# A two-block transformer kernel: 32 modulation units of the first feed-forward taken from TensorE to VectorE

## The chip, the core and the metric

The kernel runs on one core of a Trainium2 chip. The metric is device time of one execution in microseconds (us); the median of three runs is compared.

## What is computed

Two blocks follow each other, each of two layers (a mixer and a feed-forward in each), on x of 256 tokens by 1024 features, with a second stream of 256 context tokens that goes through the same mixers and the first feed-forward. Arithmetic is fp32. All shifts, scales and gates come from a condition vector by a product with a large weight matrix, the modulation; its weights are streamed once, and do not depend on x. Cut to what matters:

```python
def modulation(cond, w_ada, b_ada):
    m = jax.nn.silu(cond) @ w_ada + b_ada      # 1024 -> 6*1024, for x's condition and the context's
    return [t[..., None, :] for t in jnp.split(m, 6, axis=-1)]

def modulate(h, shift, scale):
    return h * (1 + scale) + shift

# one layer of the first block (the context takes the same path with its own condition)
h = modulate(rms_norm(x, norm1_g[i]), sh1, sc1)
x = x + g1 * (jnp.concatenate([out_a, out_b, out_c], axis=-1) @ w_out[i])
x = x + g2 * conv_ffn(modulate(rms_norm(x, norm2_g[i]), sh2, sc2), w_up[i], conv_w[i], conv_b[i], w_down[i])
```

## The kernel before

Features lie on partitions (8 tiles of 128) and tokens along the free axis. An fp32 product is made exact enough by splitting both sides into a high and a low part: ScalarE rounds a weight into wh (L238), VectorE subtracts for wl (L240), and a product is three matmuls, wh with hH, wh with hL and wl with hH (L285, L286, L289). SP issues every weight load (L219, L224). A weight of 1 MB comes as two raw halves w in two buffers; every third one of a feed-forward takes slots of a pool "x8" of 8 KB per partition instead, for its raw or its wh and wl. Three of that pool's seven slots hold xc, hcH and hcL (the context stream) during the first feed-forward; the other four are shared by such weights and by the modulation loads wm.

The first feed-forward works on x and the context together, 512 columns. It has 22 "up" steps (8 weight tiles, four runs of 24 matmuls into the PSUM tile S) and groups of 4, 4, 4, 4, 3, 3 ups with eight "down" steps each (into one of two PSUM tiles acc). After an up, VectorE and ScalarE make the convolution (L991, L993), silu and gate, and gH, gL (L1028, L1029). After a down, VectorE adds acc into x and into xc (L980, two halves).

A modulation unit (i, n) is 1 MB of the weights: two blocks k of 128 input features by 1024 of the 6144 columns of condition pair i; four units n make one of the six vectors j. mod_parts does units on TensorE: per k four matmuls (L410), the padded condition cpad (128 x 32, both conditions in it) stationary and the weights moving, 256 columns each; a sum over units in SBUF (msum, L414, L416); after the fourth unit two transposes (L426) and the bias (L428). With m=2 one call does two units. The first feed-forward does 40 units, 20 calls, in x8 tiles of 1 MB (wm, L366). The second mixers do 8 more, one per call, in half tiles mw (L372).

The order of TensorE and SP is written out in Python: steps are generators, a planner (go) lets a step's later parts follow when a planned cost has passed (yield cost, wait), and spread lays the modulation calls evenly between the main steps. VectorE, ScalarE and GpSimd are ordered by the scheduler, from what each instruction depends on. SP's issues stand in one queue: a load whose slot isn't free holds up those behind it.

Of the kernel before, what the change touches and what calls it, by code (L numbers as in the profile page):

```python
# [11 lines left out]
F32 = mybir.dt.float32  # L12
F32R = mybir.dt.float32r
BF16 = mybir.dt.bfloat16
AF = mybir.ActivationFunctionType
ALU = mybir.AluOpType
# [3 lines left out]
P = 128  # L20
D = 1024
NT = 256
KD = D // P
# [53 lines left out]
            self.pop()  # L77


def spread(main, fill):  # L80

    out, done = [], 0
    for i, u in enumerate(main):
        out.append(u)
        want = len(fill) * (i + 1) // len(main)
        out += fill[done:want]
        done = want
    return out + fill[done:]
# [17 lines left out]
class Stack:  # L106
# [293 lines left out]
    def mod_parts(self, i, n, m, then=None):  # L400


        nc = self.nc
        j, q = divmod(n, 4)
        acc = self.psum("acc", [P, 512])[:, :256]
        ks = range(2 * q, 2 * (q + m))
        ws = [w for a in range(m) for w in self.wm.pop((i, n + a))]
        for k, w in zip(ks, ws):
            for u in range(4):
                nc.tensor.matmul(acc[32 * u:32 * u + 32], lhsT=self.cpad[:, k], rhs=w[:, 256 * u:256 * u + 256],  # L410
                                 start=k == ks[0], stop=k == ks[-1])
        if q == 0:
            self.msum[i, j] = self.mp.tile([P, NT], F32, tag="msum", name="msum", bufs=1)
            nc.scalar.copy(self.msum[i, j], acc)  # L414
        else:
            nc.vector.tensor_tensor(self.msum[i, j], self.msum[i, j], acc, ALU.add)  # L416
        if then is not None:
            then()
        end = q + m == 4
        yield 0.9 * m, WAIT["mod"] if end else 0  # L420
        if not end:
            return
        sb = self.msum.pop((i, j))
        tr = self.psum("tr", [P, 2, 4, 32])
        for t in range(2):
            nc.tensor.transpose(tr[:, t].rearrange("p u v -> p (u v)"), sb[:, P * t:P * t + P], self.ident)  # L426
        b = self.sm(f"sm{i}", "b")[:, KD * j:KD * j + KD].rearrange("p (u t) -> p t u", t=2)
        nc.vector.tensor_tensor(self.mod[i][:, j].rearrange("p (u t) v -> p t u v", t=2),  # L428
                                tr[:, :, :, i // 2 * 2:i // 2 * 2 + 2],
                                b.unsqueeze(3).to_broadcast([P, 2, 4, 2]), ALU.add)  # L430
        yield 0.22, 0

    def mod_units(self, ns, m=1, x8=False, ahead=1):

        ns = ns[::m]

        def load(q):
            for a in range(m if q < len(ns) else 0):
                self.mod_load(ns[q][0], ns[q][1] + a, x8)

        def step(q):
            if q >= ahead:
                yield from self.mod_parts(*ns[q - ahead], m, lambda: load(q))
            else:
                load(q)

        def go(q):
            i, n = ns[q - ahead] if q >= ahead else (0, 0)
            self.go(step(q), f"m{i}.{n + m - 1}" if q >= ahead else None)

        return [lambda q=q: go(q) for q in range(len(ns) + ahead)]
# [254 lines left out]
    def block1(self, l, after):  # L706
        nc, key, line = self.nc, f"sm{l}", self.line
# [4 lines left out]
        t = self.x8("kvqc")  # L712
        kTB, vB = t[:, 0:512], t[:, 512:1024].rearrange("p (k c) -> p k c", k=4)
        qTC = t[:, 1024:2048].rearrange("p (s a t) -> p s a t", s=2, a=2)
        t = self.x8("kvc")
# [3 lines left out]
        u, gk = uv[:, 0], f"gn{l}"  # L719
# [17 lines left out]
        def chunk(ci, post, ss):  # L737
            return [lambda s=s: self.go(self.proj(f"win{l}", ci, s, post), f"c{ci}{s}") for s in ss]
# [6 lines left out]
        def post_bq(c):  # L745
            return lambda acc, s: self.qk(acc, 4, 64, tbq, self.sm(gk, "bq"), s == 0, rsB[:, s, :, c], 2,
                                          qTB[:, s, 2 * c:2 * c + 2])
# [177 lines left out]
        fill = self.fill_a(l)  # L925
        seq = chunk(0, post_bkv, (0,)) + chunk(1, post_bq(0), (0,)) + chunk(0, post_bkv, (1,))
        if l == 0:
            seq += chunk(1, post_bq(0), (1,))
        else:
            seq = seq[:2] + need("n1") + [self.last_loads] + seq[2:]  # L930
# [4 lines left out]
        n = len(streams)  # L935
# [10 lines left out]
        if l == 1:  # L946
            seq += [lambda: self.go(self.ctx2_norm(), "cx")]
        w0 = wouts(0, slice(0, T))
        seq += cc[:2] + need(*bnames) + spread(cc[2:], spread(w0, fill[1]))
        seq += need(*(f"g{s}" for s in streams))  # L950
        seq += need("c_0011", "c_1011")
        for a, b in MOVES[l]:
            seq.insert((a + b) % len(seq), seq.pop(a % len(seq)))
        if l == 1:
            seq = seq[:12] + spread(seq[12:], self.more_units((1, 12, 20)))
        for u_ in seq:
            u_()
        if l == 1:
# [37 lines left out]
    def ffn(self, i, T, streams, after):  # L996


        nc, key = self.nc, f"sm{i}"
# [8 lines left out]
        def up(g, j):  # L1008
            a = j - starts[g]
            if a == 0:  # L1010
                gt[g] = tuple(self.gp.tile([P, groups[g], T], F32R, tag=t, name=t) for t in ("gH", "gL"))
            wh, wl = self.weights(f"wup{i}", j, k=KD)
            ps = self.psum("S", [P, 2, 512])
            for q in streams:
                hH, hL = self.h[q]
                yield from self.mms([ps[:, b, 256 * q:256 * q + 256] for b in range(2)], range(KD),
                         lambda b, k: (wh[:, k, P * b:P * b + P], wl[:, k, P * b:P * b + P]),
                         lambda b, k: (hH[:, k], hL[:, k]))
            c = self.pt.tile([P, 2, 512], F32, tag="pt", name="cgv")
            self.conv(c[:, 0, :T], ps[:, 0, :T], key, j)  # L1020
            nc.scalar.activation(c[:, 0, :T], c[:, 0, :T], AF.Silu)
            if i < 2:
                self.conv(c[:, 1, :T], ps[:, 1, :T], key, KF + j)
                nc.vector.tensor_tensor(c[:, 1, :T], c[:, 0, :T], c[:, 1, :T], ALU.mult)
            else:
                nc.vector.tensor_tensor(c[:, 1, :T], c[:, 0, :T], ps[:, 1, :T], ALU.mult)
            gH, gL = gt[g]
            nc.scalar.copy(gH[:, a], c[:, 1, :T])  # L1028
            (nc.vector if T == 512 else nc.gpsimd).tensor_tensor(gL[:, a], c[:, 1, :T], gH[:, a].bitcast(F32), ALU.subtract)  # L1029
            if j == KF - 1:  # L1030
                self.lnexp()
# [20 lines left out]
                if last:  # L1052
                    self.post_sums(nst[0], y[:, ft], ft, i == 3)

        main = []
        for kind, g, j in self.ffn_order(T):
            if kind == "up":
                main.append(lambda g=g, j=j: self.go(up(g, j)))
            elif g < len(groups) - 1:
                main += [lambda g=g, ft=ft: self.go(down(g, ft, slice(0, T))) for ft in range(KD)]  # L1060
        for u in spread(main, self.fill_f(i)):
            u()
        if i == 0:
            self.prep1(1)
# [275 lines left out]
    def fill_f(self, i):  # L1340

        if i == 0:
            return self.more_units((1, 0, 12), (2, 0, 8), (1, 20, 24), (2, 8, 24), x8=True, m=2)
        return []

    def more_units(self, *parts, **kw):
# [279 lines left out]
```

## Time and profile before

| what | us |
|---|---|
| runs | 1751.69, 1760.24, 1749.96 |
| median | 1751.69 |
| profiled execution | 1754.48 |
| its span | 1752.7 |

The span is what the trace covers; the execution has 1.8 us more around it. Busy shares of the span are 91% for TensorE, 68% for VectorE, 50% for ScalarE and 8% for GpSimd. A busy TensorE is one with a matmul in flight, so 100% does not say that matmuls could not follow faster.

### The profile page before, as it was taken

What the parts mean: (1) busy time and instruction counts of PE and PEld (TensorE: products, weight loads), DVE (VectorE), ACT (ScalarE), POOL (GpSimd) and SP (SyncE); (2) the same over time, 40 slices, a digit from 0 to 9 for tenths busy, and PEclk for the clock granted to TensorE, in tenths of its full rate; (3) what the DMA queues carried; (4) which work ended last, traced back from release to release, by engine and by line L of the source; (5) the groups of instructions that cost most, each with busy time, mean ns of one, the idle gap of its engine ahead of it and who ended that gap; (6) DMA issues with size and microseconds to landing.
All of it is one profiled execution on the core that took longest, in us unless ns stands there. A gap on an engine that the chain in (4) does not pass through costs nothing.

```text
span 1752.7 us, 32334 instructions
## 1 busy us (share of the span) xinstructions
PE 1599.5 (91%) x12604; PEld 1419.1 (81%) x12604; DVE 1188.5 (68%) x2877; ACT 879.1 (50%) x2147; POOL 136.7 (8%) x162
## 2 busy tenths in 40 slices
PE   6999797999999999889888998988979999779997
PEld 5877457989898989788468998976869999479996
DVE  5765886755555545777788777785776567876665
ACT  6344654523242324455546656563556555656563
POOL 1000001000000000010000101000141012330110
PEclk9999998999999999999899999999989999889999
DMA  8344330444545454334334544565554546435552
GB/s 326 107 145 145 125 125 32 146 182 177 219 143 217 168 205 176 131 119 154 133 109 151 195 167 139 175 220 208 197 180 164 196 155 226 174 118 196 170 176 88
DMA packets 67402, 288.36 MB, mean 165 GB/s; under 512 B 7728, under 2 KB 9008, under 8 KB 54960
## 3 DMA queue, kind: packets, MB, share of 16 engines
q1 hardware_dynamic: 65664, 283.91, 46.0%
q10 hardware_dynamic: 1584, 2.38, 0.4%
q8 instruction: 99, 1.62, 0.4%
q14 instruction: 55, 0.45, 0.1%
HBM read 285.21 MB, written 1.05 MB: 163 GB/s over the span
## 4 chain that ended last, share of the span: by engine, by line
PE 61%; DVE 18%; DMA 10%; ACT 7%; issue 3%; POOL 1%; SPq 0%; ACTq 0%; DVEq 0%; POOLq 0%
PE S L285 9%; PE S L286 9%; PE S L289 9%; PE acc L285 8%; PE acc L286 8%; PE acc L289 8%; DVE wl L240 6%; DMA w<-in_wup_dram 5%; PE acc L410 3%; ACT wh L238 2%; DMA w<-in_wdn_dram 2%; DVE ht L529 1%; PE tr L671 1%; DMA wm<-in_wmod_dram 1%; DVE mx L661 1%
## 5 line engine op out<-in xcount | busy, mean ns | idle before, releaser
L240 DVE TENSOR_TENSOR wl<-w,wh 128x384 fp32r<-128x384 f32 (+2 forms) x1010 | 489.1, 523 | 218.5 <-ACT wh L238 190.7
L238 ACT CAST wh<-w 128x384 fp32r<-128x384 f32 (+2 forms) x1010 | 421.3, 475 | 329.4 <-DMA w<-in_wup_dram 94.9
L285 PE MATMUL S<-hH,wh 128*128 128x256 f32 x1408 | 351.3, 287 | 31.0 <-ACT hH L539 17.4
L286 PE MATMUL S<-hL,wh 128*128 128x256 f32 x1408 | 349.2, 285 | 4.7 <-POOL hL L537 4.0
L285 PEld LDWEIGHTS S<-hH,wh 128*128 128x128 f32 x1408 | 271.6, 193 | 36.9 <-ACT hH L539 18.1
L286 PEld LDWEIGHTS S<-hL,wh 128*128 128x128 f32 x1408 | 271.5, 193 | 7.1 <-POOL hL L537 5.0
L285 PE MATMUL acc<-gH,wh 128*128 128x256 f32 (+1 forms) x728 | 209.0, 311 | 9.2 <-DVE xc L980 4.8
L286 PE MATMUL acc<-gL,wh 128*128 128x256 f32 (+1 forms) x728 | 205.3, 306 | 0.0
L289 PE MATMUL S<-hH,wl 128*128 128x256 f32 x1408 | 198.4, 284 | 0.0
L289 PEld LDWEIGHTS S<-hH,wl 128*128 128x128 f32 x1408 | 182.6, 193 | 0.0
L285 PEld LDWEIGHTS acc<-gH,wh 128*128 128x128 f32 x728 | 138.9, 191 | 23.6 <-issue 7.0
L289 PE MATMUL acc<-gH,wl 128*128 128x256 f32 (+1 forms) x728 | 145.7, 306 | 0.0
L286 PEld LDWEIGHTS acc<-gL,wh 128*128 128x128 f32 x728 | 138.9, 191 | 5.5
L991 DVE SCALAR_TENSOR_TENSOR cgv<-S,sm,cgv 128x255 f32<-128x255 f32 (+1 forms) x132 | 74.8, 567 | 67.6 <-ACT cgv L988 67.1
L289 PEld LDWEIGHTS acc<-gH,wl 128*128 128x128 f32 x728 | 110.2, 191 | 6.5
L988 ACT ACTIVATE cgv<-S,sm 128x256 f32<-128x256 f32 (+1 forms) x132 | 82.7, 628 | 47.3 <-PE S L289 47.3
L285 PE MATMUL acc<-wh,hH 128*128 128x256 f32 x344 | 91.2, 296 | 10.4 <-ACT hH L539 8.2
L1029 POOL TENSOR_TENSOR gL<-cgv,gH 128x256 fp32r<-128x256 f32 x66 | 52.2, 791 | 579.5 <-ACT gH L1028 558.7
L980 DVE SCALAR_TENSOR_TENSOR x<-acc,mod,x 128x256 f32<-128x256 f32 x104 | 50.0, 482 | 57.7 <-PE acc L289 57.3
L286 PE MATMUL acc<-wl,hH 128*128 128x256 f32 x344 | 88.1, 287 | 0.0
L286 PE MATMUL S<-hcL,wh 128*128 128x256 f32 x352 | 86.5, 284 | 0.3 <-DVE hcL L540 0.3
L285 PE MATMUL S<-hcH,wh 128*128 128x256 f32 x352 | 86.4, 280 | 0.0
(268 smaller groups left out, 2837.4 us busy)
## 6 DMA issues: line engine op xcount, KB each, us to landing
wm<-in_wmod_dram SPq DMA_DIRECT2D x72, 1024.0 KB, 7.6
w<-in_wup_dram SPq DMA_DIRECT2D x140, 512.0 KB, 3.9
w<-in_wdn_dram SPq DMA_DIRECT2D x56, 512.0 KB, 4.1
mw<-in_wmod_dram SPq DMA_DIRECT2D x48, 512.0 KB, 4.7
w<-in_wup_dram SPq DMA_DIRECT2D x18, 1024.0 KB, 7.5
w<-in_win_dram SPq DMA_DIRECT2D x32, 512.0 KB, 4.0
w<-in_wout_dram SPq DMA_DIRECT2D x16, 512.0 KB, 4.7
w<-in_wqkv_dram SPq DMA_DIRECT2D x16, 512.0 KB, 3.9
```

Of the source, the lines that this page charges most:

```text
L238: self.nc.scalar.copy(h[:, c:d], w[:, c - a:d - a])
L240: self.nc.vector.tensor_tensor(l[:, c:d], w[:, c - a:d - a], h[:, c:d].bitcast(F32), ALU.subtract)
L285: mm(o, lhsT=s[0], rhs=m[0], start=k == ks[0], stop=False)
L286: mm(o, lhsT=s[0], rhs=m[1], start=False, stop=False)
L289: mm(o, lhsT=S(b, k)[1], rhs=M(b, k)[0], start=False, stop=end and k == ks[-1])
L410: nc.tensor.matmul(acc[32 * u:32 * u + 32], lhsT=self.cpad[:, k], rhs=w[:, 256 * u:256 * u + 256], start=k == ks[0], stop=k == ks[-1])
L529: nc.vector.scalar_tensor_tensor(t, self.xs[s][:, ft], A, r, ALU.mult, ALU.mult)
L661: nc.vector.tensor_reduce(mx, S[:, :, :nk], AX.X, ALU.max)
L980: self.nc.vector.scalar_tensor_tensor(x, acc[:, c], self.mods(i, j)[:, ft, s:s + 1], x, ALU.mult, ALU.add)
L988: nc.scalar.activation(out, ps, AF.Identity, scale=cw[:, n + f:n + f + 1], bias=cb[:, f:f + 1])
L991: nc.vector.scalar_tensor_tensor(o[:, :, 1:256], x[:, :, 0:255], cw[:, f:f + 1], o[:, :, 1:256], ALU.mult, ALU.add)
L1029: (nc.vector if T == 512 else nc.gpsimd).tensor_tensor(gL[:, a], c[:, 1, :T], gH[:, a].bitcast(F32), ALU.subtract)
```

## The change

Of the 48 units of the first feed-forward and the second mixers, 32 are now done on VectorE, all within the first feed-forward: (1,8) to (1,23) and (2,8) to (2,23), eight vectors j. mod_vec multiplies each 128 x 1024 block of weights by the condition's column (a number per partition) and adds it to macc, an accumulator of 128 x 1024 in three buffers that had held mw: 56 operations of VectorE (L446), and ScalarE for the first block of a vector (L444, 8 of them). Only one condition is done, the one that this vector needs. After the fourth unit the sum over partitions is made by TensorE: eight matmuls (L452) with 128 columns of macc stationary and two columns of ones moving, then the bias (L454). The planner puts them 8 us of planned cost after the step. The other 16 units stay on TensorE (8 calls of two units). The second mixers have none. spread now counts an up as 4 and a down as 1. The first feed-forward loads 48 units instead of 40. Lines up to 428 of before are one further down in after, later ones 34 to 36.

```diff
--- before.py
+++ after.py
@@ -77,12 +77,13 @@
             self.pop()
 
 
-def spread(main, fill):
-
-    out, done = [], 0
-    for i, u in enumerate(main):
+def spread(main, fill, cost=lambda u: 1):
+
+    out, done, at, all = [], 0, 0, sum(cost(u) for u in main)
+    for u in main:
         out.append(u)
-        want = len(fill) * (i + 1) // len(main)
+        at += cost(u)
+        want = len(fill) * at // all
         out += fill[done:want]
         done = want
     return out + fill[done:]
@@ -429,6 +430,41 @@
                                 tr[:, :, :, i // 2 * 2:i // 2 * 2 + 2],
                                 b.unsqueeze(3).to_broadcast([P, 2, 4, 2]), ALU.add)
         yield 0.22, 0
+
+    def mod_vec(self, i, n):
+
+
+        nc = self.nc
+        j, q = divmod(n, 4)
+        if q == 0:
+            self.msum[i, j] = self.mp.tile([P, 1024], F32, tag="mw", name="macc", bufs=3)
+        acc, v = self.msum[i, j], i // 2 * 2
+        for k, w in zip((2 * q, 2 * q + 1), self.wm.pop((i, n))):
+            if k == 0:
+                nc.scalar.activation(acc, w, AF.Copy, scale=self.cpad[:, k, v:v + 1])
+            else:
+                nc.vector.scalar_tensor_tensor(acc, w, self.cpad[:, k, v:v + 1], acc, ALU.mult, ALU.add)
+        if q < 3:
+            return
+        yield 0, 8
+        tr = self.psum("tr", [P, KD, 2])
+        for t in range(KD):
+            nc.tensor.matmul(tr[:, t], lhsT=acc[:, P * t:P * t + P], rhs=self.ones[:, 0:2], start=True, stop=True)
+        b = self.sm(f"sm{i}", "b")[:, KD * j:KD * j + KD]
+        nc.vector.tensor_tensor(self.mod[i][:, j, :, 0], tr[:, :, 0], b, ALU.add)
+        del self.msum[i, j]
+        yield 1.2, 0
+
+    def mod_vecs(self, ns):
+
+
+        def step(q):
+            if q < len(ns):
+                self.mod_load(*ns[q], True)
+            if q:
+                yield from self.mod_vec(*ns[q - 1])
+
+        return [lambda q=q: self.go(step(q), "m%d.%d" % ns[q - 1] if q else None) for q in range(len(ns) + 1)]
 
     def mod_units(self, ns, m=1, x8=False, ahead=1):
 
@@ -951,8 +987,6 @@
         seq += need("c_0011", "c_1011")
         for a, b in MOVES[l]:
             seq.insert((a + b) % len(seq), seq.pop(a % len(seq)))
-        if l == 1:
-            seq = seq[:12] + spread(seq[12:], self.more_units((1, 12, 20)))
         for u_ in seq:
             u_()
         if l == 1:
@@ -1052,13 +1086,15 @@
                 if last:
                     self.post_sums(nst[0], y[:, ft], ft, i == 3)
 
-        main = []
+        main, cost = [], {}
         for kind, g, j in self.ffn_order(T):
             if kind == "up":
                 main.append(lambda g=g, j=j: self.go(up(g, j)))
+                cost[main[-1]] = 4
             elif g < len(groups) - 1:
                 main += [lambda g=g, ft=ft: self.go(down(g, ft, slice(0, T))) for ft in range(KD)]
-        for u in spread(main, self.fill_f(i)):
+                cost.update((u, 1) for u in main[-KD:])
+        for u in spread(main, self.fill_f(i), lambda u: cost[u]):
             u()
         if i == 0:
             self.prep1(1)
@@ -1340,7 +1376,8 @@
     def fill_f(self, i):
 
         if i == 0:
-            return self.more_units((1, 0, 12), (2, 0, 8), (1, 20, 24), (2, 8, 24), x8=True, m=2)
+            return spread(self.mod_vecs([(i, n) for i in (1, 2) for n in range(8, 24)]),
+                          self.more_units((1, 0, 8), (2, 0, 8), x8=True, m=2))
         return []
 
     def more_units(self, *parts, **kw):
```

TensorE, first feed-forward, before: the end of a down (acc, 512 columns), a call of mod_parts on two units wm, and the next down.

```order
L289 MATMUL acc_6432<-gH_5526,wl_6293 128x512 x2
L410 MATMUL acc_6447<-wm_6152,cpad_103 32x256 x8
L410 MATMUL acc_6447<-wm_6154,cpad_103 32x256 x8
L285 MATMUL acc_6470<-gH_5526,wh_6292 128x512
L286 MATMUL acc_6470<-gL_5527,wh_6292 128x512
```

After, at the end of an up step (S_5983 is its PSUM tile): the column sums of macc_5642 into tr_6080, and the next up.

```order
L287 MATMUL S_5983<-hcL_3463,wh_5835 128x256
L290 MATMUL S_5983<-hcH_3462,wl_5836 128x256 x8
L452 MATMUL tr_6080<-ones_99,macc_5642 128x2 x8
L286 MATMUL S_6124<-hH_3288,wh_5969 128x256
L287 MATMUL S_6124<-hL_3289,wh_5969 128x256
```

The sum stands directly behind the up, and the next up behind the sum.

SP's queue over the same stretch of the program, before: loads of weights w and, in pairs, of modulation units wm.

```order
L224 DMA w_6008<-in_wup0_dram 128x1024
L224 DMA w_6010<-in_wup0_dram 128x1024
L366 DMA wm_6152<-in_wmod2_dram 128x2048
L366 DMA wm_6154<-in_wmod2_dram 128x2048
L224 DMA w_6156<-in_wdn0_dram 128x1024
L224 DMA w_6158<-in_wdn0_dram 128x1024
L224 DMA w_6288<-in_wdn0_dram 128x1024
L224 DMA w_6290<-in_wdn0_dram 128x1024
L224 DMA w_6414<-in_wup0_dram 128x1024
L224 DMA w_6416<-in_wup0_dram 128x1024
```

After:

```order
L367 DMA wm_5793<-in_wmod2_dram 128x2048
L367 DMA wm_5795<-in_wmod2_dram 128x2048
L225 DMA w_5831<-in_wup0_dram 128x1024
L225 DMA w_5833<-in_wup0_dram 128x1024
L367 DMA wm_5957<-in_wmod2_dram 128x2048
L367 DMA wm_5961<-in_wmod2_dram 128x2048
L225 DMA w_5965<-in_wup0_dram 128x1024
L225 DMA w_5967<-in_wup0_dram 128x1024
L367 DMA wm_6101<-in_wmod2_dram 128x2048
L225 DMA w_6106<-in_wdn0_dram 128x1024
```

The pairs have become single loads and pairs in other places, more of them between the weight loads; wm_5957, the last unit of macc_5642, goes into the slot of wh_5835, which the matmuls of S_5983 read almost to their end.

VectorE after the first group of downs, before: residual steps of downs (x, xc) and the pieces of a weight's low part wl.

```order
L980 SCALAR_TENSOR_TENSOR x_90<-acc_4275,mod0_108,x_90 128x256
L980 SCALAR_TENSOR_TENSOR xc_91<-acc_4275,mod0_108,xc_91 128x256
L980 SCALAR_TENSOR_TENSOR x_90<-acc_4294,mod0_108,x_90 128x256
L980 SCALAR_TENSOR_TENSOR xc_91<-acc_4294,mod0_108,xc_91 128x256
L980 SCALAR_TENSOR_TENSOR x_90<-acc_4309,mod0_108,x_90 128x256
L980 SCALAR_TENSOR_TENSOR xc_91<-acc_4309,mod0_108,xc_91 128x256
L240 TENSOR_TENSOR wl_4367<-w_4257,wh_4366 128x384 x2
L240 TENSOR_TENSOR wl_4367<-w_4257,wh_4366 128x256
L240 TENSOR_TENSOR wl_4367<-w_4259,wh_4366 128x384 x2
L980 SCALAR_TENSOR_TENSOR x_90<-acc_4347,mod0_108,x_90 128x256
```

After:

```order
L1014 SCALAR_TENSOR_TENSOR x_90<-acc_4264,mod0_108,x_90 128x256
L1014 SCALAR_TENSOR_TENSOR xc_91<-acc_4264,mod0_108,xc_91 128x256
L1014 SCALAR_TENSOR_TENSOR x_90<-acc_4283,mod0_108,x_90 128x256
L446 SCALAR_TENSOR_TENSOR macc_4203<-wm_4149,cpad_103,macc_4203 128x1024
L241 TENSOR_TENSOR wl_4251<-w_4153,wh_4250 128x384 x2
L241 TENSOR_TENSOR wl_4251<-w_4153,wh_4250 128x256
L241 TENSOR_TENSOR wl_4251<-w_4155,wh_4250 128x384 x2
L241 TENSOR_TENSOR wl_4251<-w_4155,wh_4250 128x256
L1014 SCALAR_TENSOR_TENSOR xc_91<-acc_4283,mod0_108,xc_91 128x256
L1014 SCALAR_TENSOR_TENSOR x_90<-acc_4298,mod0_108,x_90 128x256
L1014 SCALAR_TENSOR_TENSOR xc_91<-acc_4298,mod0_108,xc_91 128x256
```

Between the two halves of the residual of acc_4283 there now stand a step of the modulation and six pieces of a weight.

## Rows read from the trace of the kernel before

**Rows 1.** The page's busy times, whole span.
```profile
PE 1599.5 (91%) x12604; PEld 1419.1 (81%) x12604; DVE 1188.5 (68%) x2877; ACT 879.1 (50%) x2147; POOL 136.7 (8%) x162
```

**Rows 2.** Busy times by stretch: first feed-forward, its tail, second mixers; us.
```profile
330.00:690.00 360.00, 360.00 (x2894) 324.32 (x2896) 193.51 (x378) 124.86 (x262) 0.00 (x0) 1.00 0.49 181
690.00:740.00 50.00, 44.26 (x344) 35.54 (x335) 37.58 (x95) 20.45 (x47) 0.00 (x0) 0.97 0.54 201
740.00:925.00 185.00, 163.44 (x1220) 132.30 (x1220) 146.85 (x396) 99.32 (x253) 4.43 (x6) 0.93 0.39 126
```

**Rows 3.** Busy times by stretch of L410 (mod_parts' matmuls) alone.
```profile
330.00:690.00 360.00, 31.35 (x520) 15.28 (x524) 1.00 0.49 181
690.00:740.00 50.00, 7.53 (x126) 3.36 (x116) 0.97 0.54 201
740.00:925.00 185.00, 9.43 (x128) 3.52 (x128) 0.93 0.39 126
```

**Rows 4.** The same of L426 (mod_parts' transposes), first feed-forward.
```profile
330.00:690.00 360.00, 3.04 (x16) 2.09 (x16) 1.00 0.49 181
```

**Rows 5.** Chain of work that ended last, 640 to 740: start, us, what.
```profile
651.97 0.96 PE S L289 x8
652.93 1.86 PE acc L410 x32
...
705.35 9.22 DMA wm<-in_wmod_dram
714.62 1.07 PE acc L410 x16
```

**Rows 6.** VectorE groups, 330 to 690: busy us, mean ns, idle before.
```profile
L240 DVE TENSOR_TENSOR wl<-w,wh 128x384 fp32r<-128x384 f32 x112 | 59.1, 554 | 66.6 <-ACT wh L238 51.7 <-PE S L289 13.3 <-DMA w<-in_wup_dram 1.7
...
L1024 DVE TENSOR_TENSOR cgv<-cgv 128x512 f32<-128x512 f32 x21 | 14.5, 692 | 0.5
...
L416 DVE TENSOR_TENSOR msum<-msum,acc 128x256 f32<-128x256 f32 x8 | 3.3, 416 | 4.1 <-PE acc L410 4.1
```

**Rows 7.** The chain, two stretches of TensorE in the first mixers.
```profile
198.02 1.09 PE tr L783 x8
...
202.07 1.95 PE tr L834 x16
```

**Rows 8.** The page's group of 128-column weight loads.
```profile
L285 PEld LDWEIGHTS acc<-gH,wh 128*128 128x128 f32 x728 | 138.9, 191 | 23.6 <-issue 7.0
```

**Rows 9.** The chain in the second mixers.
```profile
853.90 1.86 PE acc L410 x16
...
862.86 5.47 DMA w<-in_wout_dram
```

**Rows 10.** SP's timeline in the second mixers: start, us, what it issues.
```profile
828.92 33.83 SPq L372 DMA_DIRECT2D mw<-in_wmod_dram  x6
```

**Rows 11.** Landing of the wm loads (L366), 330 to 740, min/median/max us.
```profile
DMA to landing us min/median/max: 4.7/6.9/13.7
```

**Rows 12.** What SP's queue waited for, 330 to 690: us, times, longest.
```profile
SPq L366 <- PE S L286: 74.4, 5, 17.4
```

**Rows 13.** TensorE's timeline, 286 to 310: start, us, what, idle before.
```profile
290.55 0.58 PE L285 MATMUL acc<-mixH,wh 128*128 128x256 f32 x1 [3.65 <-ACT mixH L266]
...
296.30 0.41 PE L286 MATMUL acc<-mixL,wh 128*128 128x256 f32 x1
296.51 0.41 PE L285 MATMUL acc<-mixH,wh 128*128 128x256 f32 x1
...
298.06 0.28 PE L286 MATMUL acc<-mixL,wh 128*128 128x256 f32 x1
298.18 0.28 PE L285 MATMUL acc<-mixH,wh 128*128 128x256 f32 x1
```

**Rows 14.** VectorE's timeline: two residual steps on end, 372 to 400.
```profile
378.56 0.48 DVE L980 SCALAR_TENSOR_TENSOR x<-acc,mod,x 128x256 f32<-128x256 f32 x1 [0.71 <-PE acc L289]
...
381.38 0.48 DVE L980 SCALAR_TENSOR_TENSOR x<-acc,mod,x 128x256 f32<-128x256 f32 x1 [1.34 <-PE acc L289]
```

## Prediction

> **What bounds the kernel now.** I read the busy shares first: TensorE has 91% of the span, VectorE 68% [rows 1]. Then the busy times by stretch, since the change touches three stretches only. From 330 to 690 us, the first feed-forward, TensorE is busy for 360.00 of 360 us at full granted clock, VectorE for 193.51, ScalarE for 124.86 [rows 2]: TensorE is the bound there, and whatever leaves its queue shortens the program as long as it is never kept waiting. In the tail (690 to 740) it idles for 5.7 us, in the second mixers (740 to 925) for 21.6 of 185 us [rows 2]: there chains of small steps through VectorE, ScalarE and loads bind, and work taken from TensorE counts only where it stands in such a chain.
>
> **What leaves TensorE.** L410 has 520 and 126 instructions up to 740 us, 640 of them being 20 calls of 32 [rows 3]. On the chain of work that ended last such a call takes 1.86 us, behind the last eight matmuls of an up at 0.96 [rows 5]. 12 of 20 calls go: 12 x 1.86 = 22.3 us. Of ten pairs of transposes six go; 16 of them take 3.04 us [rows 4], pipelined somewhat less, so six pairs give 1.4 to 2.3 us; I take 1.4. Together 23.7 us.
>
> **What comes to TensorE.** Eight column sums of eight matmuls each, 128 columns stationary and two moving; an fp32 matmul shows as two instructions, so 16 loads with little behind them. The trace has no such operation. The nearest: 16 instructions of L834 take 1.95 us, eight of L783 (128 columns on 128) take 1.09 us, which is 2.2 for 16 [rows 7]. Lower end: 16 of L410, with 32 columns loaded, at half a call, 0.93 [rows 5]. Upper end: 16 loads at 191 ns with no overlap, 3.1 us [rows 8]. I take 2.0, by L834, the row with as many loads of that width: 8 x 2.0 = 16 us, bounds 7 and 24. The Trainium skill (TensorE: Matmul & The Clock Gate, LDWEIGHTS) puts a load at its columns over 1.2 GHz, 107 ns for 128; by it a sum would be 1.7 us and all eight 13.7; the rows of 1.95 and 2.2 us stand above that, so it isn't used.
>
> The balance of TensorE's own work is thus 16 - 23.7, about **-8 us** (-16 to 0): most of what leaves comes back as sums.
>
> **VectorE.** The 56 new operations are 1024 wide. Forms of 256 and 512 take 416 and 692 ns [rows 6], 276 per 256, so 1024 is 692 + 2 x 276 = 1.24 us, and 56 of them 69.6 us; with the copies and adds of 12 calls gone (at most 0.42 each [rows 6], 5 us) VectorE rises from 193.51 of 360 to about 258, 72%. ScalarE gets eight copies of about the same length, 9 us onto 124.86. Neither becomes a bound as a sum. They cost where something that TensorE needs soon stands behind them in a row.
>
> **Second mixers.** Eight calls (9.43 us busy [rows 3]) and four transposes go, and 16 loads of 512 KB. On the chain there stand calls such as 1.86 us at 853.90, and a wait of 5.47 us for a w_out half [rows 9], which was issued only after six mw loads had held SP's queue for 33.83 us [rows 10]. Were all calls on the chain, 9.4 us and the wait's 5.5 would go; but the chain is mostly that of VectorE and ScalarE, where a call slips into idle time. I take five of eight calls, 5 us, and 2 of the wait (ScalarE is late next): **-7 us** (-3 to -12).
>
> **New waits.** The order of after against the durations above shows six places in the first feed-forward where TensorE must wait. It waited nowhere there.
>
> 1. After the first group of downs, one operation on wm_4149 (1.24 us) and six weight pieces (up to 0.55 each, 3.05 together [rows 6]) stand between the halves of the residual of acc_4283. The third down from there needs that buffer. VectorE needs 4.3 us and two halves; a down takes 2.81 us (378.56 to 381.38 [rows 14]). That leaves about 2.4 us with all data there; the load behind is issued only when the fourth down frees its slot, so I take 2.9.
> 2. The second group, the same with one operation between: 1.0.
> 3. The sum of macc_5076: behind its bias add stand a convolution and the next unit's step, then the six pieces of the next down's weight: 3.2.
> 4. The third group, as 1: 3.0.
> 5. The sum of macc_5642 is the surest. wm_5957 is released when the matmuls of S_5983 on wh end, and the sum stands behind that up, only the eight of 0.96 us [rows 5] between. A wm load lands after 4.7 to 6.9 us [rows 11], then two operations, 2.4 us: 4.7 + 2.4 - 1.0 = 6.1 to 8.3. I take 6.8. Before, such a release cost nothing, though the loads waited for S up to 17.4 us [rows 12], since their call stood far behind.
> 6. The sum of macc_6103: its two loads are freed by the end of a fourth down, and the sum comes 2.3 downs, 6.4 us, later; 6.9 + 2.4 and some pieces of weights make 3.7.
>
> The six are 20.6 us. The clock comes on top: after an idle time of 3.65 us matmuls at 296.30 and 296.51 still follow at 0.21 us, at 298.06 and 298.18 at 0.12 [rows 13], so about 6.5 us ran at the lower level, 1.2 GHz, and cost half of it, 3.2. That falls due after place 5 and perhaps 6. Against it, a wait gives VectorE and SP time that the next place then needn't wait for; I take off 4. **+20 us**, bounds 9 (places 5 and 6 alone, short) and 31 (each at its long end, clock twice).
>
> The tail's 9.22 us on a wm load [rows 5] may shorten, since other loads now end the stretch, or turn into one for w; I put it at nothing, between -5 and +3.
>
> **The sum.** -8 - 7 + 20 = +5 us, on the profiled execution 1754.48 to 1759.5; that execution is 2.8 above the median of the runs, 1751.69, which becomes **1757 us**. The ends: -16 - 12 + 9 - 5 = -24, and 0 - 3 + 31 + 3 = +31. Not all ends come together; the range for this case is -15 to +22, 1737 to 1774. One per cent, 17.5 us, is about what a measurement of this kernel tells from no change.
>
> **Rivals.**
>
> *The waits hardly appear* (0.22): the loads lead by more than I read, and VectorE is ahead by enough. For it: TensorE waited for no wm load in this stretch before, DMA's share is 0.49 [rows 2], and at the other six sums I found the loads early. Against: place 5 can't, by its order. With 4 us left the sum is -8 - 7 + 4 = -11, 1741; with sums at the low end -20, 1732. So the gain passes one per cent only if two bounds are met.
>
> *Slower: the x8 slots become the bound* (0.25). One place and mechanism: a unit's load waits for a slot that a matmul frees, and the sum's position is fixed by planned cost, not by the load. It decides where landing plus two operations, 7 to 9 us, is longer than what the plan puts between release and sum. I see that at two vectors of eight (places 5 and 6); if later loads queue on one another, as wm after wm in SP's order, it is so at five. Each then costs 6.4 us and some 2 of clock: 5 x 8.4 = 42 in place of places 5 and 6 with their clock, 13.7; with the other four places at 10 the sum is -15 + 42 + 10 = +37, **1789**; at four vectors 1780. The Trainium skill (TensorE: Matmul & The Clock Gate, HAM oscillation) tells of kernels in which each wait for a load drops the clock, and the matmuls after it run at half rate. By that every such vector pays, as priced; the rows after the 3.65 us agree [rows 13].
>
> *No gain in the second mixers* (0.13): the chain goes over VectorE and ScalarE whatever TensorE does, and the w_out wait turns into one for the next weight. Then -8 + 0 + 20 = +12, 1764.
>
> **How the numbers follow.** My forecast has 0.40, the rivals 0.22, 0.25 and 0.13. Faster by over 1% (under 1734): two thirds of the first rival's chance falls short of it, which leaves 0.07, and the forecast's low end adds 0.05: 0.12. Slower by over 1% (over 1769): the second rival's 0.23, of the forecast and the third 0.05: 0.28. Within: 0.60. The range takes the first rival in whole down to 1735 and reaches into the second: 1735 to 1780.
>
> **What would show it.** In the profile of after: TensorE idle 9 to 31 us between 330 and 700, most of it before L452 (waiting for VectorE's L446) and before the first matmul of a down (waiting for L1014 or L241); a lower clock just after; L452 at 1.9 to 2.2 us per 16; VectorE near 72% there; L410 256 instructions in that stretch; the second mixers shorter by 3 to 12 us. No idle there would make me wrong to the fast side; L452 waiting at most vectors, to the slow one. What I can't see is how far VectorE's and SP's rows slip together over a stretch that has become fuller for both.

## The result and the profile after

The changed kernel takes 1785.61 us (median of 4 runs, 1776.90 to 1790.83), the kernel before in the same measurement 1755.10 (4 runs, 1749.96 to 1760.24): 1.0161 times as long, 95% interval 1.0134 to 1.0188. It is slower, where 1757 with a range to 1780 was forecast. The profiled execution took 1790.83 us, the slowest of the four, and its span is 1788.9.

To see where the time went I cut the span at three instructions that both kernels have: the first convolution of the first feed-forward, the last addition into the context's residual xc, and the last normalisation product ht of the context, which ends the second mixers. Rows of those lines in the changed kernel; behind the colon are shortest, median and longest duration, then the first and the last start:

```profile
L1025 DVE SCALAR_TENSOR_TENSOR cgv<-S,sm,cgv x132: 470/482/754, 331.1 to 1736.5; 128x255 f32<-128x255 f32 x88, 128x510 f32<-128x510 f32 x44
...
L1014 DVE SCALAR_TENSOR_TENSOR xc<-acc,mod,xc x64: 467/477/489, 221.7 to 775.0; 128x256 f32<-128x256 f32 x64
...
L565 DVE SCALAR_TENSOR_TENSOR ht<-xc,mscale,rstd x32: 476/482/488, 24.2 to 945.9; 128x256 f32<-128x256 f32 x32
```

So the first feed-forward takes 443.9 us (331.1 to 775.0) and the second mixers 170.9 (to 945.9). The same cuts in the kernel before are 415.8 and 168.5: the first feed-forward has become 28.1 us longer, the second mixers have not become shorter. The rest is unchanged, 842.7 and 843.0 us; ahead of the first convolution, where nothing was changed, 5 us differ, which is chance (below).

Busy times by stretch in the changed kernel, in the columns of [rows 2]: window and length, then busy us and number of instructions of TensorE, its weight loads, VectorE, ScalarE and GpSimd, then granted clock, DMA share and GB/s:

```profile
330.00:690.00 360.00, 338.96 (x2477) 312.35 (x2477) 229.46 (x392) 123.13 (x242) 0.00 (x0) 0.97 0.54 196
690.00:760.00 70.00, 63.88 (x477) 57.28 (x476) 55.16 (x113) 27.83 (x59) 0.00 (x0) 0.95 0.51 183
760.00:950.00 190.00, 158.78 (x1054) 131.32 (x1053) 147.61 (x397) 100.42 (x254) 4.41 (x6) 0.87 0.23 76
```

TensorE, busy for all of 360 us before, is idle for 21 of them; VectorE went from 193.51 to 229.46, and the granted clock from 1.00 to 0.97. The window holds less of the stretch than before, since the stretch has become longer. Between the first two cuts, before and changed:

```profile
325.70:741.50 415.80, 410.06 (x3278) 365.66 (x3277) 235.00 (x482) 148.72 (x315) 0.00 (x0) 1.00 0.49 182
331.10:775.00 443.90, 411.92 (x3007) 378.39 (x3006) 296.52 (x538) 157.61 (x317) 0.00 (x0) 0.96 0.51 187
```

VectorE has 61.5 us more to do there, and TensorE is busy for 1.9 us longer with less work (below). Now the idle times. The timeline of TensorE in the changed kernel (start, us, what, and in brackets the idle time before it and what ended it), the eight waits of over 1.3 us before the last steps:

```profile
399.47 0.47 PE L286 MATMUL acc<-gH,wh 128*128 128x512 f32 x1 [2.08 <-DVE xc L1014]
...
457.12 0.44 PE L427 MATMUL tr<-cst,msum 128*128 128x128 f32 x2 [1.40 <-DVE msum L417]
...
534.00 1.26 PE L290 MATMUL acc<-gH,wl 128*128 128x512 f32 x2 [2.44 <-DVE wl L241]
...
557.39 0.47 PE L286 MATMUL acc<-gH,wh 128*128 128x512 f32 x1 [2.94 <-DVE xc L1014]
...
595.52 3.58 PE L452 MATMUL tr<-ones,macc 128*128 128x2 f32 x16 [7.65 <-DVE macc L446]
...
647.44 3.57 PE L452 MATMUL tr<-ones,macc 128*128 128x2 f32 x16 [3.44 <-DVE macc L446]
...
730.57 0.77 PE L286 MATMUL acc<-gH,wh 128*128 128x512 f32 x1 [4.34 <-DVE xc L1014]
...
756.12 0.39 PE L286 MATMUL acc<-gH,wh 128*128 128x256 f32 x1 [1.52 <-DVE x L1014]
```

Five of the six places of the prediction are among them, each with the wait that it named: 2.08 at place 1; 2.44 at 3; 2.94 at 4; 7.65 at 5 and 3.44 at 6. In the group of place 2 the wait for xc is a short one of 0.52 (462.29); the 1.40 there stands before a pair of mod_parts' transposes, which waits for VectorE's sum msum and was not forecast. The last two rows, 4.34 and 1.52, are in the tail group of downs, for which the prediction had put nothing. With two short ones (0.52, 0.56) and the 4.82 us ahead of the last down group (4.83 before as well) the idle time is 31.7 us where it was 5.7.

What TensorE's clock did after the longest wait, in windows of 8 us (column before the last two: granted clock):

```profile
586.00:594.00 8.00, 1.87 (x16) 1.67 (x14) 3.82 (x5) 2.08 (x3) 0.00 (x0) 0.91 0.71 284
594.00:602.00 8.00, 6.48 (x30) 6.48 (x31) 4.94 (x9) 4.04 (x8) 0.00 (x0) 0.50 0.68 241
602.00:610.00 8.00, 8.00 (x66) 8.00 (x65) 4.21 (x8) 0.00 (x0) 0.00 (x0) 0.95 0.80 280
```

For 8 us the granted clock is 0.50, the lower of the two levels, 1.2 GHz. Behind the waits of 2.08, 2.44, 2.94, 3.44 and 4.34 us:

```profile
397.00:405.00 8.00, 5.92 (x37) 5.09 (x36) 6.37 (x12) 1.05 (x3) 0.00 (x0) 1.00 0.93 321
...
533.00:541.00 8.00, 7.00 (x22) 5.42 (x23) 6.79 (x15) 2.42 (x5) 0.00 (x0) 0.79 0.40 131
...
556.00:564.00 8.00, 6.61 (x23) 5.34 (x24) 5.63 (x13) 2.47 (x6) 0.00 (x0) 0.79 0.90 314
...
647.00:655.00 8.00, 7.56 (x28) 6.74 (x29) 4.28 (x11) 2.57 (x5) 0.00 (x0) 0.57 0.88 325
...
729.00:737.00 8.00, 6.43 (x18) 5.09 (x19) 6.81 (x14) 2.93 (x6) 0.00 (x0) 0.57 0.66 229
```

The sum behind the longest wait shows what the lower level makes of it. The chain of work that ended last has sums at both levels, and mod_parts' calls at the price of [rows 5]:

```profile
481.90 1.68 PE tr L452 x16
...
503.76 1.86 PE acc L411 x32
...
528.84 1.69 PE tr L452 x16
...
595.52 3.58 PE tr L452 x16
...
647.44 3.57 PE tr L452 x16
```

VectorE's new operations between 330 and 690 us, 47 of the 56 (form, count, busy us, mean ns, idle before):

```profile
L446 DVE SCALAR_TENSOR_TENSOR macc<-wm,cpad,macc 128x1024 f32<-128x1024 f32 x47 | 60.2, 1281 | 12.6 <-DMA wm<-in_wmod_dram 12.2 <-ACT macc L444 0.2
```

And what SP's queue waited for from 330 to 735 us (us, times, longest): loads of units (L367) stood behind matmuls on weights for 103 us, in nine waits of up to 24.7 us. Before it had been 74.4 us behind S [rows 12] and 31 behind acc, without harm. So the queue does not wait longer for such slots than before; what can differ is how soon the loads are needed, and slots8 and beforeslots below test that.

```profile
SPq L225 <- DVE wl L241: 177.6, 42, 19.3
SPq L367 <- PE acc L287: 59.8, 4, 24.7
SPq L367 <- PE S L287: 43.5, 5, 18.7
```

The acc line before:

```profile
SPq L366 <- PE acc L286: 31.2, 4, 7.8
```

### The profile page after: what moved, and what is told of

Its sections match the earlier page's. It is cut to its first block, busy times and chain, and to the rows that moved or that the text cites. A ratio compares the mean times of both kernels' runs of the same rounds, so it can differ in the third digit from the quotient of the medians.

```text
span 1788.9 us, 31546 instructions
## 1 busy us (share of the span) xinstructions
PE 1605.9 (90%) x12204; PEld 1438.1 (80%) x12204; DVE 1247.5 (70%) x2921; ACT 890.1 (50%) x2149; POOL 138.8 (8%) x162
## 4 chain that ended last, share of the span: by engine, by line
PE 41%; DVE 16%; DMA 9%; ACT 6%; issue 3%; POOL 0%; SPq 0%; ACTq 0%; DVEq 0%; POOLq 0%
PE S L286 7%; PE S L287 7%; PE S L290 7%; DVE wl L241 6%; PE acc L286 5%; PE acc L287 5%; PE acc L290 5%; DMA w<-in_wup_dram 4%; DMA w<-in_wdn_dram 2%; ACT wh L239 2%; DMA wm<-in_wmod_dram 2%; DVE ht L565 1%; DMA w<-in_wqkv_dram 1%; PE acc L411 1%; DVE macc L446 1%
## 5 line engine op out<-in xcount | busy, mean ns | idle before, releaser
L286 PE MATMUL acc<-wh,hH 128*128 128x256 f32 x344 | 92.0, 298 | 10.3 <-ACT hH L575 8.1
```

Source lines behind the costliest of these rows:

```text
L286: mm(o, lhsT=s[0], rhs=m[0], start=k == ks[0], stop=False)
```

## The experiments

The theories. A: what counts are sums that stand too early for their last load, and unit steps in VectorE's row between the halves of a residual. B: VectorE simply has too much to do there. F, formed after the first runs: both are passed on from the loads of the units, which wait in SP's row for an x8 slot that a weight's matmuls hold. For the second mixers, C: the calls taken away had kept TensorE's clock up; D: the chain there never ran over them.

Ratios are to runs of the kernel before on the same chip. The table has each kernel's stretches by the three cuts, from its own profile, and TensorE's idle time in the first feed-forward (sum of the timeline's waits of 0.3 us and more).

| kernel | time, ratio to before (95%) | first feed-forward us | idle us | second mixers us |
|---|---|---|---|---|
| before | 1755.1 | 415.8 | 5.7 | 168.5 |
| again (before once more) | 1764.8, one run | 416.9 | 6.6 | 171.0 |
| after | 1.0161 (1.0134 to 1.0188) | 443.9 | 31.7 | 170.9 |
| late | 1.0106 (1.0071 to 1.0141) | 434.1 | 24.4 | 168.3 |
| narrow | 1.0095 (1.0060 to 1.0130) | 429.4 | 20.3 | 169.1 |
| fillmix | 1.0185 (1.0151 to 1.0220) | 443.6 | 31.8 | 169.4 |
| mixff | 1.0036 (1.0008 to 1.0064) | 427.3 | 8.3 | 164.8 |
| actpool | 1.0344 (1.0287 to 1.0401) | 485.6 | 59.2 | 164.9 |
| costonly | 1761.7, one run | 414.5 | 4.8 | 170.3 |
| resident | 1745.0, one run | 404.4 | 5.8 | 168.5 |
| noroom | 0.9989 (0.9963 to 1.0015) | 407.2 | 11.5 | 169.2 |
| noroom2 | 0.9963 (0.9940 to 0.9986) | 409.9 | 13.3 | 169.3 |
| slots8 | 0.9964 (0.9932 to 0.9996) | 408.4 | 9.4 | 172.2 |
| beforeslots | 1.0026 (1.0005 to 1.0047) | 419.2 | 10.5 | 171.3 |

**late**: the sums later.

```diff
-        yield 0, 8
+        yield 0, 24
         tr = self.psum("tr", [P, KD, 2])
```

> Only the planned time between the last unit of a vector and its column sum is changed, from 8 to 24 us. Theory A (a sum that stands too early for its last load): the two waits of 7.65 and 3.44 us before L452 and the half clock behind them go, two sums take 1.7 instead of 3.6 us; 15 to 20 us less than the changed kernel, about 1768, ratio to before 1.006 to 1.010. Rival B (VectorE has too much to do in the first feed-forward): the waits come back before the downs, 0 to 5 us less, 1781 to 1786.

The two waits before L452 are gone, and 10 us (1.0161 to 1.0106), about half of what theory A gave. The waits before downs stayed, and one behind mod_parts' sum grew (timeline of TensorE, late):

```profile
398.66 0.77 PE L286 MATMUL acc<-gH,wh 128*128 128x512 f32 x1 [2.25 <-DVE xc L1014]
...
458.55 0.44 PE L427 MATMUL tr<-cst,msum 128*128 128x128 f32 x2 [2.18 <-DVE msum L417]
...
538.70 1.27 PE L290 MATMUL acc<-gH,wl 128*128 128x512 f32 x2 [3.29 <-DVE wl L241]
...
719.95 0.77 PE L286 MATMUL acc<-gH,wh 128*128 128x512 f32 x1 [3.89 <-DVE xc L1014]
```

After the wait of 2.18 us at 458.55 the granted clock of the next 8 us is 0.62:

```profile
450.00:458.00 8.00, 6.37 (x63) 4.69 (x61) 6.17 (x12) 2.52 (x5) 0.00 (x0) 1.00 0.56 165
458.00:466.00 8.00, 7.45 (x29) 6.61 (x30) 5.88 (x14) 4.11 (x9) 0.00 (x0) 0.62 0.91 360
```

So waits of 2 us can cost clock too, though not each does: behind the 2.08 us of the changed kernel, and in late behind a wait of 2.94 us at 563.82, the granted clock stayed at 1.00.

```profile
563.00:571.00 8.00, 7.18 (x38) 6.17 (x39) 6.20 (x14) 2.47 (x6) 0.00 (x0) 1.00 0.95 351
```

The two waits that are gone were 11.1 us, but the idle time fell by 7.3 only: the others have grown by 3.8 in sum. The place of the sums explains a third of the loss (9.8 of 28.1 us in the first feed-forward), no more.

**narrow**: VectorE's multiply-adds on 128 of 1024 columns, seven eighths of the product left out.

```diff
-                nc.vector.scalar_tensor_tensor(acc, w, self.cpad[:, k, v:v + 1], acc, ALU.mult, ALU.add)
+                nc.vector.scalar_tensor_tensor(acc[:, :128], w[:, :128], self.cpad[:, k, v:v + 1], acc[:, :128], ALU.mult, ALU.add)
```

> The changed kernel with VectorE's 56 multiply-adds on 128 columns instead of 1024 (so seven eighths of the product are left out); loads, sums and order stay. VectorE has some 54 us less to do in the first feed-forward. Theory A (loads released late, sums placed too early): the wait at macc_5642 stays at 5 us or more, the one at macc_6103 shrinks, and the waits before downs halve: 8 to 15 us less than the changed kernel, 1771 to 1778. Rival B (VectorE's load): all waits of the first feed-forward fall under 2 us in sum, 30 us less, about 1755.

1771.39 us, as theory A said: with VectorE's steps at 349 instead of 1281 ns half of the loss stays, and the wait at the sum of macc_5642 is still 5.79 us, since a load is what it waits for (timeline, narrow):

```profile
587.10 3.57 PE L452 MATMUL tr<-ones,macc 128*128 128x2 f32 x16 [5.79 <-DVE macc L446]
```

Rival B falls as the whole cause.

**fillmix**: eight calls back in the second mixers, without loads, their results unused.

```diff
+                nc.tensor.matmul(acc[32 * u:32 * u + 32], lhsT=self.cpad[:, k],
+                                 rhs=self.blank[:, 256 * u:256 * u + 256], start=k == 0, stop=k == 1)
...
+        if l == 1:
+            seq = seq[:12] + spread(seq[12:], [lambda q=q: self.go(self.idle_unit(q), None) for q in range(8)])
```

> The changed kernel with eight calls of 8 matmuls (128 x 32 stationary, 256 columns) put back into the second mixers, on a constant tile, without loads and with their results unused. Theory C (the calls kept TensorE's clock up there): granted clock from 760 to 950 rises from 0.87 towards 0.93, and the stretch from the last residual of the first feed-forward to the context's last normalisation, 170.9 us now and 168.5 before, is 2 to 6 us shorter in spite of more work. Rival D (the chain runs over VectorE and ScalarE): the stretch is the same or up to 5 us longer, whatever the clock does.

The granted clock from the second cut to the third rose from 0.87 to 0.92, but late had 0.92 there without any such call; the stretch is 169.4 us, within what the others without calls show. Theory C is not borne out: with the calls and the clock back, no gain is seen. Nor is a cost, as D says, but the kernels without calls scatter by 7 us here (below), so one profile can't show that the calls are free.

**mixff**: the kernel before, the mixers' eight units done by TensorE in the first feed-forward.

```diff
-            seq = seq[:12] + spread(seq[12:], self.more_units((1, 12, 20)))
...
-            return self.more_units((1, 0, 12), (2, 0, 8), (1, 20, 24), (2, 8, 24), x8=True, m=2)
+            return self.more_units((1, 0, 24), (2, 0, 24), x8=True, m=2)
```

> The kernel before, with the eight units of the second mixers done by TensorE in the first feed-forward (24 calls of two units there, none in the mixers). Four more calls of 1.86 us cost 7.4 us there. By the prediction's term the mixers give 7 back: ratio 1.000. By the trace of the changed kernel they give nothing or lose 2: ratio 1.004 to 1.006, 1762 to 1765.

The ratio is 1.0036, just under the second figure; its interval (1.0008 to 1.0064) leaves out the first, 1.000. In the profile the first feed-forward is 11.5 us longer and the mixers 3.7 shorter. That looks like half of the predicted gain, but the nine kernels without calls in the mixers lie between 164.8 and 172.2 us, mean 168.6, and the four with them (before, again, costonly, beforeslots) between 168.5 and 171.3, mean 170.3. The gain is about 2 us, from nothing to 4 by this scatter, and no single profile can show it. TensorE's idle time between these cuts scatters less: 25.7 to 27.9 us in the nine, 21.6 to 23.8 in the four, 21.2 in fillmix. So some 4 us of the calls' 9.4 had stood in time that is idle without them. The granted clock there is lower without calls, 0.90 on the average against 0.92 or 0.93 in each of the four, which takes back more.

**actpool**: late, with the products by ScalarE and the additions by GpSimd.

```diff
-                nc.vector.scalar_tensor_tensor(acc, w, self.cpad[:, k, v:v + 1], acc, ALU.mult, ALU.add)
+                nc.scalar.activation(w, w, AF.Copy, scale=self.cpad[:, k, v:v + 1])
+                nc.gpsimd.tensor_tensor(acc, acc, w, ALU.add)
```

> As late, but VectorE has no part in the units: ScalarE multiplies each block in place (56 times some 1.15 us), GpSimd adds it to the accumulator (56 times, some 3 us by the slope of its 256-column adds at 0.79 us). Theory A (a unit's step and its load stand in VectorE's row between the halves of a residual): the waits before downs, 12.9 us in late, go for the most part, and the clock's falls behind them; the first feed-forward 415 to 422 us instead of 434, the whole about 1757 to 1760. Rival E (the x8 slots and SP's row of loads hold everything up): waits of 10 us and more stay, 430 us and over, 1770.

Neither: 1820.59 us, the worst of all. VectorE has none of the units' work, but what it has became slower while GpSimd adds; its pieces of weights, 554 ns in [rows 6], take 737 on the average (groups of actpool by form, 330 to 740). In the trace those that overlap none of GpSimd's additions take 551 ns, the 17 that do 1712 on the average.

```profile
L447 POOL TENSOR_TENSOR macc<-macc,wm 128x1024 f32<-128x1024 f32 x50 | 124.2, 2484 | 305.5 <-ACT wm L446 296.0 <-issue 7.8
...
L241 DVE TENSOR_TENSOR wl<-w,wh 128x384 fp32r<-128x384 f32 x106 | 75.2, 737 | 41.7 <-ACT wh L239 25.0 <-POOL macc L447 16.7
```

Theory A can't be judged by this run, since it brings a cost of its own: waits for wl of up to 5.62 us.

**costonly**: the kernel before with the new weighting of spread (the hunks at spread and at its call in the diff of the change). **again**: the kernel before without an edit.

> The kernel before with only the new weighting of spread (an up counts 4, a down 1). Theory A: nothing is done by VectorE, no wait in the first feed-forward over 1 us, its stretch within 3 us of 415.8. Rival: the weighting puts calls between ups, where their loads or buffers are late, and costs 5 us or more by itself.

> The kernel before, once more, for what varies by itself: the first convolution at 325.7 us in its first profile and at 331 to 332 in all profiles of changed kernels so far, though nothing is changed ahead of it. If that is chance, it comes at 331 here too; the first feed-forward takes 415 to 417 us, the second mixers 167 to 171.

The weighting costs nothing, 414.5 us. And the first convolution comes at 331.8 us in the kernel before too:

```profile
L991 DVE SCALAR_TENSOR_TENSOR cgv<-S,sm,cgv x132: 467/482/751, 331.8 to 1710.1; 128x255 f32<-128x255 f32 x88, 128x510 f32<-128x510 f32 x44
```

So the 5 us ahead of the stretch were chance of the first profile, and they are no part of the change.

**resident**: the changed kernel without VectorE's 32 loads; the steps read hH, so the units' values are meaningless.

```diff
-                self.mod_load(*ns[q], True)
+                self.wm[ns[q]] = [self.h[0][0].rearrange("p k t -> p (k t)")[:, 1024 * e:1024 * e + 1024].bitcast(F32) for e in range(2)]
```

> The changed kernel without its 32 loads of units for VectorE: the multiply-adds read a tile of the hidden state that is there anyway, so these units' values are not the reference's; all instructions of the engines stay. Theory F (what hurts are the loads and the slots they wait for, VectorE's row only passes the wait on): idle of TensorE in the first feed-forward falls from 31.7 us to under 12, its stretch from 443.9 to 410 to 416. Rival B (VectorE's own time, 72 us more): idle stays at 20 us or more, the stretch at 428 or more.

Theory F, and more clearly than expected: all of VectorE's 56 steps are there at their full length, and the idle time is that of the kernel before, 5.8 us. All of TensorE's waits ahead of the last down group (333 to 730 us):

```profile
PE acc L286 <- DVE xc L1014: 0.6, 1, 0.6
PE tr L427 <- DVE msum L417: 0.4, 1, 0.4
PE acc L286 <- DVE x L1014: 0.2, 1, 0.2
```

So the waits before downs came from the loads as well. The stretch is 404.4 us against 415.8 with the same idle time: TensorE's own work has become 11.4 us less.

**noroom** and **noroom2**: late, with the x8 slots left to the units; noroom2 also loads a unit two steps ahead.

```diff
-            plan[n] = name, off, size, extra and (n - base) % 3 == 0, cut
+            plan[n] = name, off, size, extra and (n - base) % 3 == 0 and name[0] not in ("wup0", "wdn0"), cut
```

> As late, and no weight of the first feed-forward takes x8 slots, so the four free slots belong to the units alone and no load of a unit waits for a matmul on a weight; the weights have two buffers of each kind only. Theory F: the waits before downs that come from a late unit go, the first feed-forward 418 to 426 us instead of 434.1, ratio 1.001 to 1.006. Rival G (the weights need the third buffer): TensorE waits for wl or wh instead, 434 us or more.

> As noroom, with a unit loaded two steps ahead of its work instead of one, so that it has landed when VectorE comes to it. Theory F: a few us less again than noroom, 412 to 422 us, ratio 0.998 to 1.004. Rival G: as in noroom, no gain.

Both took the whole loss back, more than either expectation gave: 407.2 and 409.9 us. Loading further ahead adds nothing in the stretch.

**slots8**: the changed kernel with that one line, sums at 8 us. **beforeslots**: the kernel before with it.

> The changed kernel with one edit: no weight of the first feed-forward takes x8 slots; the sums keep their 8 us. Theory F (the slots are the cause, the sums' place only passes it on): loads of units wait for no matmul, so the sums of macc_5642 and macc_6103 no longer wait, the first feed-forward takes 407 to 415 us, ratio 0.996 to 1.002. Rival A (the sums' place counts by itself): a wait of 3 us or more stays before at least two sums, 418 us or more, ratio 1.003 or more.

> The kernel before with the same edit of the slots and nothing else. If the shared slots cost the kernel before nothing, as its trace without waits says, it stays at 414 to 418 us in the first feed-forward, ratio 0.998 to 1.002, and what noroom2 gains comes from the units on VectorE. If it gains as much as noroom2 (ratio under 0.997), the gain is one of the slots alone.

One line brings 1785.61 to 1751.13 us, and the kernel is faster than the one before (0.9964, 0.9932 to 0.9996). No sum waits for a load any more; TensorE's waits are nearly all before downs, the longest the 4.2 ahead of the last down group, which every kernel has, and loads of units wait for no weight's matmul (waits of TensorE, 330 to 740, and of SP's queue, 330 to 735, in slots8):

```profile
PE acc L286 <- DVE xc L1014: 9.7, 8, 4.2
...
SPq L225 <- DVE wl L241: 304.7, 60, 13.8
SPq L367 <- DVE macc L446: 10.9, 7, 2.4
```

The kernel before gains nothing from the same line, 1.0026 (1.0005 to 1.0047): it paid nothing for the shared slots. So what slots8 gains is no gain of the slots alone, nor one of fewer loads, since it has all of them. The expectation's lower rival, a sum that counts by its place, falls: with the slots apart the place at 8 us costs nothing.

## Why the prediction was wrong

The places of the waits, the main uncertainty of the prediction, were right, nearly to the size: 2.9, 1.0, 3.2, 3.0, 6.8 and 3.7 us, sum 20.6, against 2.08, 1.92 (1.40 and a short one of 0.52), 2.44, 3.50 (0.56 and 2.94), 7.65 and 3.44, sum 21.0. That the sums agree so closely is in part luck: the 1.40 is a wait that was not forecast, and single places are off by up to 0.9. The steps that failed are others.

1. **The clock** was put at 3.2 us, due after place 5 and perhaps 6. The stretch is 28.1 us longer; idle time has grown by 26.0, and TensorE's own work fell by 12 calls at 1.86 and six pairs at 0.23, 23.7 us, against eight sums at 1.68, 13.4: -10.3 us. That leaves 28.1 - 26.0 + 10.3 = 12.4 us for the clock. It is a remainder, but the trace's record of the clock agrees: between the cuts TensorE was busy at the lower level for 30.0 us, and for 3.4 in the kernel before; half of the difference is 13.3 us (an estimate, as if all of that work ran at half rate). The lower level stood not only behind the two sums but behind the waits of places 3 and 4 and of the tail, 2.4 to 4.3 us long, each time for some microseconds, and in late behind one of 2.18. I had read one wait of 3.65 us [rows 13] and charged the long places alone. This was the term most off, by 9 us.

2. **Take off 4**, because a wait gives the next place time: the six came out at 21.0, their sum without it. Why is not shown. That each load hangs on a slot which TensorE itself frees, and so is late wherever TensorE stands, would explain it; but in late, with 11.1 us of waits taken out, the others are 3.8 longer, which speaks for some giving, though the sums have moved there too. 4 us.

3. **The tail at nothing**: 4.34 and 1.52 us of new waits before downs of the last groups, 6 us. The load of 9.22 us [rows 5] had little to give back: TensorE had waited for it for 0.86 us.

```profile
714.62 1.07 PE L410 MATMUL acc<-wm,cpad 128*32 128x256 f32 x16 [0.86 <-DMA wm<-in_wmod_dram]
```

4. **The second mixers at -7**: about -2, by the means above. The w_out wait did shrink, from 5.3 to 1.0 us of ScalarE's waiting from the second to the third cut, but TensorE's wait for the softmax (Pm) at the same step grew; in again and in the changed kernel (timeline of TensorE):

```profile
856.92 2.08 PE L849 MATMUL S<-kvc,kvqc 32*128 32x512 f32 x4 [2.83 <-ACT Pm L817]
```

```profile
885.31 2.08 PE L885 MATMUL S<-kvc,kvqc 32*128 32x512 f32 x4 [4.72 <-ACT Pm L853]
```

"ScalarE is late next" was written there, yet two thirds of the calls were still counted as gain. 5 us.

On the other side the sums were cheaper than taken, 1.68 and not 2.0 us at the full clock, 2.6 us in all (and the two at 3.6 are in the clock's term). The estimate of 1.7 us a sum from the Trainium skill (TensorE: Matmul & The Clock Gate, LDWEIGHTS), which the prediction set aside, was the better one: 1.68 and 1.69 measured. The steps of VectorE were as worked out, 1.28 against 1.24 us.

In sum: 9 + 4 + 6 + 5 - 2.6 = 21 us above the 5 forecast, so 26. The medians differ by 30.5, and the interval of the ratio is 23.5 to 33 us, so this agrees. The two stretches of the first profiles give 30.5 as well (28.1 and 2.4); there the 4.4 over 26 are the second mixers of that one profile, 170.9 us where the means let -2 be expected.

**The rival** that gave 1789 named the x8 slots as the bound. The cause is shown: without loads (resident), or with slots of their own for them (slots8), the loss is gone. Its size came another way: not five vectors with a long wait before their sum but two, and the rest as short waits before downs, where a step of VectorE or a weight's pieces waited for a load in the same row. It had 0.25; the prediction saw the mechanism and priced it by the count of long waits.

What the first rival, hidden waits, took for this kernel comes about in slots8: 408.4 us, 7.4 less than 415.8 with 3.7 us more of idle time, so TensorE's own work fell by 11 us, as in resident, where the balance had -8.

How the six places split between load and order is not fully settled. late shows that a sum's place matters while loads are late, slots8 that it doesn't when they are not; both agree with F. narrow gave back 14.5 us of 28.1, so shorter steps also help while loads are late. Nor is it separated how much came from a unit's own late load and how much from the weights' loads that stood behind it in SP's row; slots8 removes both.

## What to carry to other kernels

Work moved from the bounding engine to an idle one brings its data's buffers with it: look at which instruction frees the slot of each new load, and if that is one of the bounding engine, the load starts late by design, whatever share of DMA or VectorE is free. Then ask how soon after the landing the bounding engine needs what comes of it: here the queue had waited as long before, and it cost nothing. Price the waits that this makes on TensorE with the clock behind them, here about half of their sum again. And a gain in a stretch where the bounding engine already idles should be counted at nothing until the chain without that work has been followed step by step.

## What was not expected of the hardware

- With GpSimd adding 128 x 1024 values (2484 ns each), VectorE's subtractions of 128 x 384 took 737 ns instead of 554 on the average: 551 where no addition overlapped them, 1712 on the average where one did.
- A wait of 2.18 us (late) was followed by a granted clock of 0.62 over 8 us, one of 2.94 in the same run by 1.00: the length of the wait alone does not tell. The same sum of 16 loads took 1.68 us at the upper level and 3.58 at the lower.
- The stretch of the second mixers differed by 7 us (164.8 to 172.2) among nine kernels whose code there is the same, and its granted clock between 0.86 and 0.92.
